# A decoder layer in split fp32r: the low parts of every fourth weight block formed by an accumulating transfer instead of VectorE

## The chip, the cores and the metric

One core of one Trainium2 chip runs the whole program. Its engines are TensorE (PE, matrix multiply; PEld is its weight load), VectorE (DVE), ScalarE (ACT), GpSimd (POOL) and SyncE (SP), which share an on-chip memory (SBUF); TensorE accumulates into PSUM banks. SP, ACT and POOL can each issue DMA transfers, which run on the core's 16 DMA engines. Every engine works through its own instructions in order and waits on semaphores for the others. The metric is the device time of one execution in microseconds (us).

## The reference

One layer of a decoder trunk with a sequence of 256 tokens, model width 2048, all in float32. The part that the change touches is the second half: a gated MLP and a gated embedding, both on RMS-normalised rows.

```python
h = rms_norm(x, mix_norm_g[i])
z = h @ w_in[i]
...
x = x + jnp.concatenate([ha, hb], axis=-1) @ w_out[i]
h = rms_norm(x, ffn_norm_g[i])
u = h @ w_up[i]
a, g = jnp.split(u, 2, axis=-1)
a = causal_dwconv(a, conv_w[i], conv_b[i])
x = x + (jax.nn.gelu(a, approximate=False) * g) @ w_down[i]
gate = jax.nn.sigmoid(rms_norm(x, ple_norm_g[i]) @ w_ple_gate[i])
x = x + gate * (p[i].astype(x.dtype) @ w_ple_proj[i])
```

The weights of these four products are `w_up` (2048 x 11264), `w_down` (5632 x 2048), `w_ple_gate` (2048 x 2048) and `w_ple_proj` (256 x 2048).

## The kernel before

Each weight matrix is streamed once from HBM in blocks of 128 partitions x 1024 float32 values (512 KB). To keep float32 accuracy on TensorE in its float32r format, each block is split in two: `hi` is the block rounded to float32r, `lo = raw - hi` is what the rounding left. The activations are split the same way (`split_T`, lines 139 to 149). A product is then three matmuls: hi times hi, lo times hi, hi times lo.

Two runs of `run_stream` (line 209) carry the whole layer: the first from `w_in` to `w_out`, the second from the up projection to the end. The second has 301 blocks: 176 of `w_up`, 88 of `w_down`, and 37 of `w_ple_proj` and `w_ple_gate`. For a block j the steps are

- SP loads it into a buffer `raw` (line 222), up to three blocks ahead in the loop (`AHEAD_DMA`),
- ACT writes `hi` (line 237), VectorE writes `lo` (line 239), up to three blocks ahead of TensorE (`AHEAD_SPLIT`),
- TensorE multiplies: `wide_group` (lines 317 and 318, the up projection), `token_group` (lines 267 to 269, the down projection, the gate and the projection of p), or `feature_group` (lines 293 to 295, first stream only).

The buffers set the pace of the look-ahead. There are three `raw` buffers (`RAW`) and four each of `hi` and `lo` (`PARTS`). A `raw` buffer comes free when both parts of its block have been formed; a `hi` or `lo` buffer when TensorE has finished its block. Which free buffer a new block gets, and the order of the instructions on each engine, are decided when the program is built, by a scheduler that estimates when each comes free; SP issues the loads strictly in the order of the blocks.

In the up projection a group of 8 blocks fills four PSUM banks; ACT and VectorE empty them (`merge`, `up_a`, `up_g`) between the splits of later blocks. The 22 groups each have a pair of offsets from the table `OFFS`: so many elements are the `hi` and the `lo` of its blocks shifted inside their buffers, which are 128 elements (`SLACK`) longer than a block. All other blocks have offset zero.

Of the kernel before, what the change touches and what calls it, by code (L numbers as in the profile page):

```python
# [10 lines left out]
F32R = mybir.dt.float32r  # L11
AF = mybir.ActivationFunctionType
ALU = mybir.AluOpType
AX = mybir.AxisListType

P = 128
# [7 lines left out]
FF = 5632  # L24
# [8 lines left out]
BLK = 1024  # L33
RAW, PARTS = 3, 4
AHEAD_DMA, AHEAD_SPLIT = 3, 3
PAD = 48
SLACK = 128

OFFS = [(0, 16), (16, 0), (0, 32), (16, 16), (0, 48), (32, 32), (0, 64), (16, 32), (48, 48), (0, 80), (32, 0),
        (0, 96), (16, 48), (64, 64), (0, 112), (64, 0), (8, 8), (32, 48), (48, 16), (64, 80), (8, 24), (0, 8)]  # L40


@with_exitstack
def layer_kernel(
# [7 lines left out]
    act, dve, pe, pool = nc.scalar, nc.vector, nc.tensor, nc.gpsimd  # L52
# [4 lines left out]
    wp = ctx.enter_context(tc.tile_pool(name="w", bufs=3))  # L57
# [5 lines left out]
    def f32(ap):  # L63
        return ap.bitcast(F32)
# [125 lines left out]
    def traced():  # L190

        return nc.cur_bb.bb.instructions[-1]
# [5 lines left out]
    def pull(n):  # L198

        while n > 0 and side:  # L200
            turn[0] ^= 1
            job = side[min(turn[0], len(side) - 1)]
            try:
                next(job)
                n -= 1
            except StopIteration:
                side.remove(job)

    def run_stream(blocks, pulls, ramp=False):

        nb = len(blocks)
        raws, parts = {}, {}
        split = 0
        for i in range(-AHEAD_DMA, nb):
            j = i + AHEAD_DMA
            if j < nb:
                src, _, _, load = blocks[j][:4]
                if load is not None:
                    load()
                kb, n = src.shape[1], src.shape[2]  # L220
                raws[j] = wp.tile([P, BLK], F32, tag="raw", name=f"raw{j}", bufs=RAW)
                nc.sync.dma_start(out=raws[j][:, : kb * n].rearrange("p (k n) -> p k n", k=kb), in_=src)

            ahead = min(AHEAD_SPLIT, 1 + i // 2) if ramp else AHEAD_SPLIT
            while i >= -1 and split < min(nb, i + ahead + 1):
                j, split = split, split + 1
                src, _, prep, _ = blocks[j][:4]
                if prep is not None:
                    prep()
                kb, n = src.shape[1], src.shape[2]  # L230
                w = kb * n
                raw = raws.pop(j)
                hi = wp.tile([P, BLK + SLACK], F32R, tag="hi", name=f"hi{j}", bufs=PARTS)
                lo = wp.tile([P, BLK + SLACK], F32R, tag="lo", name=f"lo{j}", bufs=PARTS)
                oh, ol = blocks[j][4] if len(blocks[j]) > 4 else (0, 0)
                hi, lo = hi[:, oh : oh + w], lo[:, ol : ol + w]
                act.copy(hi, raw[:, :w])  # L237
                last["hi"] = traced()
                dve.tensor_sub(lo, raw[:, :w], f32(hi))  # L239
                parts[j] = [v.rearrange("p (k n) -> p k n", k=kb) for v in (hi, lo)]  # L240
            if i >= 0:
                blocks[i][1](*parts.pop(i))
                pull(pulls)

    def wsrc(w, k0, kb, c0, n):
        return w[0, k0 * P : (k0 + kb) * P, c0 : c0 + n].rearrange("(k p) n -> p k n", p=P)
# [30 lines left out]
    def feature_group(w, c0, actT, finish):  # L277


        st = {}  # L280
        blocks = []
        for k0 in range(0, KD, 2):
            def fn(hi, lo, k0=k0):
                if k0 == 0:
                    st["b"] = [bank("mm", f"fg{j}").rearrange("p (j s) -> p j s", j=2) for j in range(2)]
                for j in range(4):
                    o = st["b"][j // 2][:, j % 2, :]
                    cols = slice(j * P, (j + 1) * P)
                    for i in range(2):
                        a = actT()[:, k0 + i, :]  # L290
                        first = k0 == 0 and i == 0 and j % 2 == 0
                        last = k0 == KD - 2 and i == 1 and j % 2 == 1
                        pe.matmul(o, hi[:, i, cols], a[:, 0:256], start=first, stop=False)  # L293
                        pe.matmul(o, hi[:, i, cols], a[:, 256:512], start=False, stop=False)  # L294
                        pe.matmul(o, lo[:, i, cols], a[:, 0:256], start=False, stop=last)  # L295
                    if k0 == KD - 2 and j % 2 == 1:
                        finish(j // 2, st["b"][j // 2])
            blocks.append((wsrc(w, k0, 2, c0, 512), fn, None, None))
        return blocks

    def wide_group(w, c0, actT, finish, tag, offs):


        st = {}
        blocks = []
        for k0 in range(0, KD, 2):
            def fn(hi, lo, k0=k0):
                if k0 == 0:
                    st["b"] = [bank(tag, f"wg{j}") for j in range(4)]
                for j in range(4):  # L310
                    o = st["b"][j]
                    cols = slice(j * P, (j + 1) * P)
                    for i in range(2):
                        a = actT()[:, k0 + i, :]
                        first = k0 == 0 and i == 0
                        last = k0 == KD - 2 and i == 1
                        pe.matmul(o, hi[:, i, cols], a, start=first, stop=False)  # L317
                        pe.matmul(o[:, 256:512], lo[:, i, cols], a[:, 0:256], start=False, stop=last)  # L318
                    if k0 == KD - 2:
                        finish(j, o)  # L320
            blocks.append((wsrc(w, k0, 2, c0, 512), fn, None, None, offs))
        return blocks

    apool = ctx.enter_context(tc.tile_pool(name="acts", bufs=1))
# [9 lines left out]
    with tc.tile_pool(name="mix", bufs=1) as mp:  # L334
# [328 lines left out]
        blocks = []  # L663
# [58 lines left out]
    with tc.tile_pool(name="ffn", bufs=1) as fp:  # L722
# [10 lines left out]
        def up_a(q):  # L733
            st = {}

            def f(jj, b):
                pair, j = divmod(jj, 2)
                if j == 0:
                    st["a"] = fp.tile([P, 2, S], F32, tag="a", name="a", bufs=2)
                    st["c"] = gl[q, pair] = fp.tile([P, 2, S], F32, tag="gl", name="c", bufs=3)  # L740
                a, c, k = st["a"], st["c"], 4 * q + jj
                merge(a[:, j], b)
                dve.tensor_mul(a[:, j], a[:, j], rb)
                act.activation(c[:, j], a[:, j], AF.Identity, scale=cT[:, 88 + k : 89 + k],
                               bias=cT[:, 132 + k : 133 + k])
                for d in (1, 2):
                    dve.scalar_tensor_tensor(out=c[:, j, d:S], in0=a[:, j, 0 : S - d],
                                             scalar=cT[:, 88 - 44 * d + k : 89 - 44 * d + k],
                                             in1=c[:, j, d:S], op0=ALU.mult, op1=ALU.add)
                if j == 1:  # L750
                    act.activation(c, c, AF.Gelu)
                    dve.tensor_mul(c, c, rb2)
            return f

        def up_g(q):
            st = {}

            def f(jj, b):
                pair, j = divmod(jj, 2)
                if j == 0:  # L760
                    st["u"] = fp.tile([P, 2, S], F32, tag="a", name="u", bufs=2)
                u, k = st["u"], 4 * q + 2 * pair
                merge(u[:, j], b)
                if j == 1:
                    dve.tensor_mul(u, u, gl.pop((q, pair)))
                    split_T(uT[:, k : k + 2, :], u)
            return f

        blocks = []
        x2 = aT["cur"]  # L770
        for q in range(KF // 4):
            blocks.extend(wide_group(w_up, q * 512, lambda: x2, up_a(q), "mm", OFFS[2 * q]))
            blocks.extend(wide_group(w_up, FF + q * 512, lambda: x2, up_g(q), "aux", OFFS[2 * q + 1]))
        ssq3 = sm.tile([P, NT, 4], F32, name="ssq3")
        x3T = {}

# [30 lines left out]
        for c0, n in ((0, 512), (512, 512), (1024, 512), (1536, 256), (1792, 256)):  # L807
            blocks.extend(token_group(w_ple_proj, [0], lambda: pT, c0, n, proj_done, tag="aux"))
            blocks.extend(token_group(w_ple_gate, all_k, get_x3T, c0, n, gate_done(c0, n, c0 == 1792)))
        run_stream(blocks, 0)  # L810


# [28 lines left out]
```

## Time and profile before

| | us |
|---|---|
| median of 2 runs (1292.0 to 1293.0) | 1292.5 |
| the profiled execution, whole | 1292.68 |
| its span, first to last instruction | 1291.0 |
| up projection, from 450.6 to 944.2 in the span | 493.6 |
| down projection, 944.2 to 1186.2 | 242.0 |
| gate, projection of p and the end, 1186.2 to 1291.0 | 104.8 |

The granted TensorE clock is 0.999 over the span. The span is one profiled execution; the 1.7 us between it and the whole lie around the program. All rows below come from that execution. Times in a row are microseconds unless marked ns; "x" and a number is a count of instructions; after a bar stand the busy time and the mean ns of one, and after the next bar the idle time of the engine just before them, with what ended it behind "<-".

### The profile page before, as it was taken

What the parts mean: (1) busy time and instruction counts of PE and PEld (TensorE: products, weight loads), DVE (VectorE), ACT (ScalarE), POOL (GpSimd) and SP (SyncE); (2) the same over time, 40 slices, a digit from 0 to 9 for tenths busy, and PEclk for the clock granted to TensorE, in tenths of its full rate; (3) what the DMA queues carried; (4) which work ended last, traced back from release to release, by engine and by line L of the source; (5) the groups of instructions that cost most, each with busy time, mean ns of one, the idle gap of its engine ahead of it and who ended that gap; (6) DMA issues with size and microseconds to landing.
All of it is one profiled execution on the core that took longest, in us unless ns stands there. A gap on an engine that the chain in (4) does not pass through costs nothing.

```text
span 1291.0 us, 18150 instructions
## 1 busy us (share of the span) xinstructions
PE 1284.0 (99%) x7060; PEld 1123.9 (87%) x7060; DVE 754.6 (58%) x1008; ACT 650.0 (50%) x964; POOL 18.4 (1%) x33
## 2 busy tenths in 40 slices
PE   9999999999999999999999999999999999999998
PEld 7899999988888888888888888888888888888888
DVE  5455566554565575766676576667654545455554
ACT  7655455435554464555455455545543434444443
POOL 2000000000000000000000000000000000000000
PEclk9999999999999999999999999999999999999999
DMA  8676755556655666666666666666656665565663
GB/s 248 175 189 188 217 151 144 159 144 171 177 184 185 186 180 194 184 191 184 192 190 185 188 188 185 190 187 190 191 193 191 191 192 186 193 191 192 203 204 123
DMA packets 132039, 238.69 MB, mean 185 GB/s; under 512 B 7945, under 2 KB 28017, under 8 KB 131953
## 3 DMA queue, kind: packets, MB, share of 16 engines
q1 hardware_dynamic: 131072, 237.07, 62.0%
q8 instruction: 55, 0.90, 0.3%
q10 hardware_dynamic: 657, 0.43, 0.1%
q0 software_dynamic: 224, 0.03, 0.1%
q14 instruction: 31, 0.25, 0.1%
HBM read 235.40 MB, written 2.10 MB: 184 GB/s over the span
## 4 chain that ended last, share of the span: by engine, by line
PE 98%; DMA 1%; DVE 0%; ACT 0%; issue 0%; SPq 0%; DVEq 0%
PE wg L317 25%; PE tg L268 17%; PE tg L269 17%; PE tg L267 17%; PE wg L318 13%; PE fg L293 2%; PE fg L295 2%; PE fg L294 2%; DMA raw<-in_w_in_dram 1%; PE xT L155 1%; PE mob L610 0%; PE msc L584 0%; PE qkp L508 0%; PE sc L524 0%; PE ob L549 0%; PE rowb L495 0%
## 5 line engine op out<-in xcount | busy, mean ns | idle before, releaser
L239 DVE TENSOR_TENSOR lo<-raw,hi 128x1024 fp32r<-128x1024 f32 (+2 forms) x462 | 546.7, 1184 | 478.4 <-ACT hi L237 476.1
L237 ACT CAST hi<-raw 128x1024 fp32r<-128x1024 f32 (+2 forms) x462 | 470.2, 1018 | 563.8 <-PE tg L269 283.2
L317 PE MATMUL wg<-x2T,hi 128*128 128x512 f32 x1408 | 492.5, 394 | 0.0
L318 PE MATMUL wg<-x2T,lo 128*128 128x256 f32 x1408 | 394.8, 281 | 0.0
L317 PEld LDWEIGHTS wg<-x2T,hi 128*128 128x128 f32 x1408 | 264.4, 188 | 60.9
L318 PEld LDWEIGHTS wg<-x2T,lo 128*128 128x128 f32 x1408 | 265.5, 189 | 0.1
L267 PE MATMUL tg<-hi,uT 128*128 128x512 f32 x352 | 137.2, 390 | 0.0
L269 PE MATMUL tg<-hi,uT 128*128 128x512 f32 x352 | 137.0, 389 | 0.0
L268 PE MATMUL tg<-lo,uT 128*128 128x512 f32 x352 | 137.0, 389 | 0.0
L268 PE MATMUL tg<-lo,hT 128*128 128x512 f32 (+1 forms) x384 | 136.6, 356 | 0.2 <-DVE lo L239 0.2
L267 PE MATMUL tg<-hi,hT 128*128 128x512 f32 (+1 forms) x384 | 136.0, 358 | 0.0
L269 PE MATMUL tg<-hi,hT 128*128 128x512 f32 (+1 forms) x384 | 135.6, 354 | 0.0
L268 PEld LDWEIGHTS tg<-lo,hT 128*128 128x128 f32 x384 | 72.2, 188 | 7.9 <-DVE lo L239 0.7
L269 PEld LDWEIGHTS tg<-hi,hT 128*128 128x128 f32 x384 | 72.1, 188 | 7.5
L267 PEld LDWEIGHTS tg<-hi,hT 128*128 128x128 f32 x384 | 71.8, 188 | 7.2 <-ACT hT L146 0.3
L269 PEld LDWEIGHTS tg<-hi,uT 128*128 128x128 f32 x352 | 66.1, 188 | 13.7
L267 PEld LDWEIGHTS tg<-hi,uT 128*128 128x128 f32 x352 | 66.1, 188 | 13.6
L268 PEld LDWEIGHTS tg<-lo,uT 128*128 128x128 f32 x352 | 66.1, 188 | 13.6
L293 PE MATMUL fg<-hT,hi 128*128 128x256 f32 x256 | 74.7, 292 | 0.0
L295 PE MATMUL fg<-hT,lo 128*128 128x256 f32 x256 | 73.1, 285 | 0.0
L294 PE MATMUL fg<-hT,hi 128*128 128x256 f32 x256 | 72.8, 284 | 0.0
L268 PE MATMUL tg<-lo,x3T 128*128 128x512 f32 (+1 forms) x160 | 55.5, 347 | 0.0
(212 smaller groups left out, 1186.6 us busy)
## 6 DMA issues: line engine op xcount, KB each, us to landing
raw<-in_w_up_dram SPq DMA_DIRECT2D x176, 512.0 KB, 4.2
raw<-in_w_down_dram SPq DMA_DIRECT2D x88, 512.0 KB, 4.8
raw<-in_w_in_dram SPq DMA_DIRECT2D x79, 512.0 KB, 3.8
raw<-in_w_in_dram SPq DMA_DIRECT2D x48, 344.0 KB, 3.4
raw<-in_w_out_dram SPq DMA_DIRECT2D x32, 512.0 KB, 4.2
raw<-in_w_ple_gate_dram SPq DMA_DIRECT2D x32, 512.0 KB, 4.8
xs<-in_x_dram SPq DMA_DIRECT2D x8, 256.0 KB, 7.8
raw<-in_w_ple_proj_dram SPq DMA_DIRECT2D x3, 512.0 KB, 4.7
```

The source lines that it names most:

```text
L155: pe.transpose(bk[:, t * P : (t + 1) * P], xs[:, t, k * P : (k + 1) * P], ident)
L237: act.copy(hi, raw[:, :w])
L239: dve.tensor_sub(lo, raw[:, :w], f32(hi))
L267: pe.matmul(o, ah, hi[:, i, :], start=first, stop=False)
L268: pe.matmul(o, ah, lo[:, i, :], start=False, stop=False)
L269: pe.matmul(o, al, hi[:, i, :], start=False, stop=last)
L293: pe.matmul(o, hi[:, i, cols], a[:, 0:256], start=first, stop=False)
L294: pe.matmul(o, hi[:, i, cols], a[:, 256:512], start=False, stop=False)
L295: pe.matmul(o, lo[:, i, cols], a[:, 0:256], start=False, stop=last)
L317: pe.matmul(o, hi[:, i, cols], a, start=first, stop=False)
L318: pe.matmul(o[:, 256:512], lo[:, i, cols], a[:, 0:256], start=False, stop=last)
```

## The change

From the up projection on, in every fourth block (j % 4 == 3, 75 of the 301), `lo` is formed without VectorE: ACT writes it a second time from `raw`, with scale -1 into float32r, which gives -hi; then POOL issues a transfer that adds `raw` onto it in SBUF. The other blocks are split as before. The table of offsets goes: `hi` always starts at the front of its buffer, which loses its slack, and `lo` is shifted by 16 elements in all blocks of `wide_group` and `feature_group`, and by none in those of `token_group`.

```diff
-SLACK = 128
...
-OFFS = [(0, 16), (16, 0), (0, 32), (16, 16), (0, 48), (32, 32), (0, 64), (16, 32), (48, 48), (0, 80), (32, 0),
...
+LO_SHIFT = 16
...
-    def run_stream(blocks, pulls, ramp=False):
+    def run_stream(blocks, pulls, ramp=False, by_dma=False):
...
-                hi = wp.tile([P, BLK + SLACK], F32R, tag="hi", name=f"hi{j}", bufs=PARTS)
-                lo = wp.tile([P, BLK + SLACK], F32R, tag="lo", name=f"lo{j}", bufs=PARTS)
-                oh, ol = blocks[j][4] if len(blocks[j]) > 4 else (0, 0)
-                hi, lo = hi[:, oh : oh + w], lo[:, ol : ol + w]
+                hi = wp.tile([P, BLK], F32R, tag="hi", name=f"hi{j}", bufs=PARTS)
+                lo = wp.tile([P, BLK + 128], F32R, tag="lo", name=f"lo{j}", bufs=PARTS)
+                hi, lo = hi[:, :w], lo[:, shift : shift + w]
                 act.copy(hi, raw[:, :w])
                 last["hi"] = traced()
-                dve.tensor_sub(lo, raw[:, :w], f32(hi))
+                if by_dma and j % 4 == 3:
+                    act.activation(lo, raw[:, :w], AF.Copy, scale=-1.0)
+                    pool.dma_start(out=lo, in_=raw[:, :w], accum_op=ALU.add)
+                else:
+                    dve.tensor_sub(lo, raw[:, :w], f32(hi))
...
-        run_stream(blocks, 0)
+        run_stream(blocks, 0, by_dma=True)
```

The instructions move at three places that matter. In the rows that follow, a number behind an underscore is a buffer's running name; in brackets stand the semaphores waited for: DMAHW and a digit is the landing of a transfer of SP's, DMASW and a digit that of one of POOL's, DVE, PE and Activation the progress of that engine.

SP's queue in the middle of the up projection, before:

```order
L222 DMA raw83_6458<-in_w_up_dram 128x2x512 [waits DMAHW6_49,DVE_49]
L222 DMA raw84_6484<-in_w_up_dram 128x2x512 [waits DMAHW7_49,DVE_49]
L222 DMA raw85_6506<-in_w_up_dram 128x2x512 [waits DMAHW0_49,DVE_49]
L222 DMA raw86_6528<-in_w_up_dram 128x2x512 [waits DMAHW1_49,DVE_49]
L222 DMA raw87_6550<-in_w_up_dram 128x2x512 [waits DMAHW2_49,DVE_49]
```

The same place of SP's queue in the change:

```order
L222 DMA raw83_6478<-in_w_up_dram 128x2x512 [waits DMAHW5_49,DMASW2_49]
L222 DMA raw84_6505<-in_w_up_dram 128x2x512 [waits DMAHW7_49,DVE_49]
L222 DMA raw85_6527<-in_w_up_dram 128x2x512 [waits DMAHW0_49,DVE_49]
L222 DMA raw86_6549<-in_w_up_dram 128x2x512 [waits DMAHW2_49,DVE_49]
L222 DMA raw87_6571<-in_w_up_dram 128x2x512 [waits DMAHW1_49,DMASW3_49]
```

Nothing changed its place, but the load of block 83 now waits for the landing of POOL's transfer of block 79 (lane 2) and that of block 87 for block 83's (lane 3), since they reuse those blocks' `raw` buffers. In 32 of the 44 such rounds of the up projection it is the load of block d+4 that waits for the transfer of block d, in 12 that of block d+3.

SP's queue in the down projection, in the change (before, each of these rows waits for a load's landing and DVE):

```order
L222 DMA raw202_9401<-in_w_down_dram 128x2x512 [waits DMAHW5_49,DMASW0_49,Activation_49]
L222 DMA raw203_9419<-in_w_down_dram 128x2x512 [waits DMAHW6_49,DVE_49]
L222 DMA raw204_9438<-in_w_down_dram 128x2x512 [waits DMAHW7_49,DVE_49]
L222 DMA raw205_9456<-in_w_down_dram 128x2x512 [waits DMAHW0_49,DVE_49]
L222 DMA raw206_9474<-in_w_down_dram 128x2x512 [waits DMAHW1_49,DMASW1_49,Activation_49]
```

Here, and in most rounds behind it, it is the load of block d+3 (202 for 199, 206 for 203) that waits, and the load of block d+4, itself one of the changed blocks, stands right behind it in the queue.

TensorE at block 83 of the up projection, before:

```order
L317 MATMUL wg0_6464<-x2T_3856,hi83_6460 128x512 [waits Activation_49]
L318 MATMUL wg0_6464<-x2T_3856,lo83_6461 128x256 [waits DVE_49]
L317 MATMUL wg0_6464<-x2T_3856,hi83_6460 128x512
L318 MATMUL wg0_6464<-x2T_3856,lo83_6461 128x256
L317 MATMUL wg1_6465<-x2T_3856,hi83_6460 128x512
```

TensorE at the same block in the change:

```order
L321 MATMUL wg0_6485<-x2T_3856,hi83_6480 128x512 [waits Activation_49]
L321 MATMUL wg1_6486<-x2T_3856,hi83_6480 128x512
L321 MATMUL wg2_6487<-x2T_3856,hi83_6480 128x512
L321 MATMUL wg3_6488<-x2T_3856,hi83_6480 128x512
L322 MATMUL wg0_6485<-x2T_3856,lo83_6481 128x256 [waits DMASW3_49]
```

The first matmul that reads the block's `lo` now waits for the landing of POOL's transfer, and one to three matmuls on `hi` of the other banks have moved ahead of it.

More of the change, by code (lines that the diff above doesn't have):

```diff
@@ L36 @@
 PAD = 48
-SLACK = 128
-OFFS = [(0, 16), (16, 0), (0, 32), (16, 16), (0, 48), (32, 32), (0, 64), (16, 32), (48, 48), (0, 80), (32, 0),
-        (0, 96), (16, 48), (64, 64), (0, 112), (64, 0), (8, 8), (32, 48), (48, 16), (64, 80), (8, 24), (0, 8)]
+LO_SHIFT = 16
 @with_exitstack
@@ L226, in run_stream @@
                 j, split = split, split + 1
-                src, _, prep, _ = blocks[j][:4]
+                src, _, prep, _, *shift = blocks[j]
+                shift = shift[0] if shift else 0
                 if prep is not None:
@@ L297, in fn, with wide_group @@
                         finish(j // 2, st["b"][j // 2])
-            blocks.append((wsrc(w, k0, 2, c0, 512), fn, None, None))
+            blocks.append((wsrc(w, k0, 2, c0, 512), fn, None, None, LO_SHIFT))
         return blocks
-    def wide_group(w, c0, actT, finish, tag, offs):
+    def wide_group(w, c0, actT, finish, tag):
         st = {}
@@ L320, in fn @@
                         finish(j, o)
-            blocks.append((wsrc(w, k0, 2, c0, 512), fn, None, None, offs))
+            blocks.append((wsrc(w, k0, 2, c0, 512), fn, None, None, LO_SHIFT))
         return blocks
@@ L771, in layer_kernel @@
         for q in range(KF // 4):
-            blocks.extend(wide_group(w_up, q * 512, lambda: x2, up_a(q), "mm", OFFS[2 * q]))
-            blocks.extend(wide_group(w_up, FF + q * 512, lambda: x2, up_g(q), "aux", OFFS[2 * q + 1]))
+            blocks.extend(wide_group(w_up, q * 512, lambda: x2, up_a(q), "mm"))
+            blocks.extend(wide_group(w_up, FF + q * 512, lambda: x2, up_g(q), "aux"))
         ssq3 = sm.tile([P, NT, 4], F32, name="ssq3")
```

## The prediction

> **What bounds the kernel now.** I read the page first (busy shares, then the chain of work that ended last), then the busy time by stage, then who waits for whom, then the transfers.
>
> ```profile
> PE 1284.0 (99%) x7060; PEld 1123.9 (87%) x7060; DVE 754.6 (58%) x1008; ACT 650.0 (50%) x964; POOL 18.4 (1%) x33
> PE 98%; DMA 1%; DVE 0%; ACT 0%; issue 0%; SPq 0%; DVEq 0%
> ```
>
> TensorE is busy 99% of the span and carries 98% of the chain. VectorE, which the change relieves, is busy 58% and has no share of the chain. So nothing is gained by doing its work elsewhere; the question is only whether TensorE is still fed.
>
> ```profile
> 450.60:944.20 493.60, 493.60 (x2829) 432.50 (x2828) 331.33 (x467) 263.66 (x358) 0.69 (x1) 1.00 0.65 188
> 944.20:1186.20 242.00, 242.00 (x1082) 200.63 (x1081) 119.84 (x115) 102.54 (x115) 0.00 (x0) 1.00 0.60 191
> 1186.20:1291.00 104.80, 100.56 (x550) 87.62 (x548) 54.24 (x64) 44.55 (x54) 0.70 (x1) 0.99 0.55 178
> ```
>
> These are the three stages of the second stream: length, then busy time of PE, PEld, DVE, ACT and POOL, the granted clock, the share and rate of the transfers. The up projection takes 493.6 / 176 = 2.80 us a block, the down projection 242.0 / 88 = 2.75 us; I take 2.75 us for the last stage too. Four blocks, one round of the change, are 11.2 us, then 11.0 us. That is the time in which the feeding must go round once.
>
> ```profile
> ACT hi L237 <- PE wg L317: 199.3, 154, 2.0
> SPq L222 <- DVE lo L239: 797.1, 363, 5.5
> 664.53 1.05 ACT L237 CAST hi<-raw 128x1024 fp32r<-128x1024 f32 x1 [1.00 <-PE wg L317]
> 667.30 1.05 ACT L237 CAST hi<-raw 128x1024 fp32r<-128x1024 f32 x1 [1.72 <-PE wg L317]
> 665.62 1.22 DVE L239 TENSOR_TENSOR lo<-raw,hi 128x1024 fp32r<-128x1024 f32 x1 [0.95 <-ACT hi L237]
> ```
>
> The waits (total, times, longest) show how the feeding turns today: ACT waits for TensorE to free a `hi` buffer, SP waits for VectorE to finish a `lo` and so free a `raw`. The timeline (start, duration) gives the steps: `hi` 1.05 us, 0.04 us of handing over, `lo` 1.22 us. A block's parts are ready about 2.3 us after TensorE frees their buffers, and TensorE comes to them three blocks, 8.4 us, later: 6.1 us of slack.
>
> **The change, part by part.** First its transfers, as the trace of before shows their kin: median us from issue to landing, then the load queue's total, then least, median and greatest for all loads of line 222.
>
> ```profile
> raw<-in_w_up_dram SPq DMA_DIRECT2D x176, 512.0 KB, 4.2
> raw<-in_w_down_dram SPq DMA_DIRECT2D x88, 512.0 KB, 4.8
> raw<-in_w_ple_gate_dram SPq DMA_DIRECT2D x32, 512.0 KB, 4.8
> g<-in_mix_norm_g_dram ACTq DMA_DIRECT2D x1, 8.0 KB, 2.5
> vrows<-in_ffn_norm_g_dram POOLq DMA_DIRECT2D x1, 8.0 KB, 3.5
> 1.41 0.69 POOL L94 DMA_DIRECT2D vrows<-in_ffn_norm_g_dram  x1 [0.32 <-issue]
> q1 hardware_dynamic: 131072, 237.07, 62.0%
> DMA to landing us min/median/max: 2.9/4.1/6.9
> ```
>
> *The landing of the new transfer, L.* No transfer of before adds, and none from POOL is large, so L is unknown. POOL's first transfer needs 3.5 us for 8 KB, of which POOL itself is busy 0.69 us; ACT's of 8 KB needs 2.5 us. The loads' own pace is 237.07 MB / (0.62 x 1291 us) = 0.296 MB per us, so 512 KB (0.524 MB) take 1.77 us. One pass over the data gives 3.5 + 1.77 = 5.3 us; a second pass, to fetch what is added onto, gives 7.0; a third 8.8. From below, a plain load of the same size lands in 4.2 us. I take 6.1 us, between one pass and two: the bytes don't come from HBM, but there are twice as many to read, and the loads run beside them at a share of 0.60 to 0.65. The ends 4.2 and 8.8 go into the range.
>
> The Trainium skill, "Collectives: The Full Stack" (The bandwidth ceiling: the fold count and why AG ≠ RS ≠ AR), says that an add in the DMA engines isn't slowed by the adding but by its two source reads on one queue, which halves the rate. No transfer of this trace tests that. By it L would be 7.0 us; what the sum becomes stands below as a rival.
>
> *Where L lies on the path.* The landing of block d frees its `raw` buffer, and SP holds the load that waits for it and all behind it. In 32 of the 44 rounds of the up projection that is the load of d+4, the next changed block. It closes a ring: landing of d, load of d+4 (4.2), `hi` (1.05), the negated copy on ACT (priced as the `hi` that reads and writes the same shapes, 1.05), five handovers of 0.04 (0.2), transfer L. One turn is 4.2 + 1.05 + 1.05 + 0.2 + 6.1 = 12.6 us, against TensorE's 11.2. Slack can't help a ring: each turn is late by the difference, so after the 6 us of slack are used, TensorE waits in every turn. In the other 12 rounds the load of d+3 waits and d+4's comes behind it, 1.77 us later: 14.4 us. In the down projection nearly all rounds are of that kind, with 4.8 us a load: 4.8 + 1.77 + 2.1 + 0.2 + 6.1 = 15.0 us against 11.0. In the last stage likewise.
>
> *The sum against the profiled execution.* Up: 32 x 12.6 + 12 x 14.4 = 576 us; in half of the 44 rounds a bank's copy (0.37 us, row below) stands on ACT between `hi` and the negated copy, 22 x 0.37 = 8; together 584, less 493.6: +90. Down: 22 x 15.0 = 330, less 242.0: +88. Last stage: 9 x (15.0 - 11.0) = +36. Sum +214 on 1292.7 us (0.2 us above the median): 1507 us.
>
> ```profile
> L730 ACT COPY a<-wg 128x256 f32<-128x256 f32 x44 | 16.3, 370 | 5.7 <-PE wg L318 5.7
> L239 DVE TENSOR_TENSOR lo<-raw,hi 128x1024 fp32r<-128x1024 f32 x296 | 362.5, 1225 | 315.4 <-ACT hi L237 313.9
> L237 ACT CAST hi<-raw 128x1024 fp32r<-128x1024 f32 x176 | 184.8, 1050 | 210.3 <-PE wg L317 199.1 <-ACT uT L143 6.9 <-issue 2.1
> ```
>
> *VectorE.* 75 x 1.225 = 92 us go; all of it lies beside TensorE, so 0. *ACT.* 75 x 1.05 = 79 us come, in its idle time (210 us before `hi` in the up projection alone); they count only in the ring above. What stands behind the negated copy is the next `hi`, which has slack. *POOL.* 75 issues of about 0.7 us; its only other work here is two tiny steps; the 0.7 is inside L. *The matmuls moved ahead* let TensorE begin a changed block on `hi` alone; they don't shorten the ring: 0. *Transfers.* One added transfer per four loads raises the bytes moved by a quarter to a half, so the share of 0.65 would go to about 0.81 to 0.97 at the old pace; it doesn't bound at the slower one.
>
> *The offsets.* Five groups of eight blocks of the up projection, the third, fourth, fifteenth, twenty-first and last:
>
> ```profile
> 496.50:518.70 22.20, 22.20 (x65) 12.03 (x65) 1.00 0.67 190
> 518.70:541.30 22.60, 22.60 (x65) 12.02 (x65) 1.00 0.66 185
> 765.70:788.10 22.40, 22.40 (x65) 12.03 (x65) 1.00 0.65 189
> 899.90:922.10 22.20, 22.20 (x66) 12.03 (x65) 1.00 0.65 190
> 922.10:944.20 22.10, 22.10 (x65) 11.88 (x64) 1.00 0.60 184
> ```
>
> With (0, 32), (16, 16), (0, 112), (8, 24) and (0, 8) a group takes 22.1 to 22.6 us; the mean is 493.6 / 22 = 22.4. One pair for all can win 22 x 0.3 = 7 us or lose 22 x 0.2 = 4. I take 0, since the ring leaves TensorE idle anyway.
>
> **The rivals.** *The ring stays inside TensorE's round, and nothing changes.* In the down projection it needs 8.9 + L below 11.0, so L below 2.1; for a loss within 2% (26 us; about what a measurement of this kernel can tell from no change) 31 x (8.9 + L - 11.0) = 26, so L up to 2.9. For it: the bytes stay on the chip. Against it: 2.9 us is the fastest load on record, and POOL's 8 KB took 3.5. It gives 1292 to 1318 us. 6 in 100. *Faster* would need TensorE itself to run faster; the offsets can give 7 us, 0.5%. 1 in 100 for more than 2%.
>
> *The adding reads twice and has no overlap, L = 7.0*: the turns grow by 0.9 us, 75 x 0.9 = 68, so 1575 us. For it: nothing shows that the second read is free. Against it: the 1.77 us is a rate from HBM. This is what the rule of the Trainium skill named above ("Collectives: The Full Stack") would make of it. 20 in 100.
>
> *The transfer is slow, L of 9 us and more*, because the add or POOL's writing of its steps costs more than passes over the data. With L = 12 every turn grows by 5.9 us: 75 x 5.9 = 443, so 1950 us. For it: no row has an add. Against it: POOL's issues cost only about 0.7 us. 13 in 100.
>
> **How the numbers follow.** The forecast, a ring paced by L of about 6, has 60 in 100: 1507 us. Its lower end, L = 4.2: the up projection loses only in the 12 long rounds, 12 x (12.5 - 11.2) = 16, the down projection 22 x (13.1 - 11.0) = 46, the last stage 19: 1374 us. Its upper end, L = 8.8: 75 x 2.7 = 203 more, 1710 us. The two-read case lies inside. The range 1375 to 1740 takes in the beginning of the slow case (L = 9.2) and leaves out some 19 in 100. Slower by over 2%: 60 + 20 + 13 = 93 in 100; within 2%: 6; faster: 1.
>
> **What would show it.** Right: in the profile of the changed kernel TensorE is idle some 200 us, all of it in the second stream, ahead of matmuls on `lo` and put down to POOL's transfer; SP waits for that transfer; a round lasts about 12.6 us in the up projection and 15 in the down projection; the transfer's row says 5.3 to 7. The first stream, to 450 us, is unchanged. The step on the order of loads is wrong if the down projection loses no more per round than the up projection; the price of L is wrong if its row lies outside 4.2 to 8.8. The whole is wrong if TensorE stays at 99% with rounds of 11 us: then the landing is below 3 us, or the load behind it isn't held.

## The result and the profile after

| | before | after |
|---|---|---|
| median, us | 1292.5 | 1392.35 (1390.8 to 1393.9) |
| ratio, 95% interval | | 1.0774 [1.0752, 1.0795] |
| the profiled execution: whole, span | 1292.68, 1291.0 | 1393.89, 1392.2 |

The change made the kernel 100 us slower. The forecast, 1507 us, had the direction, the place and the mechanism; it had the size at twice what came.

First the page of the kernel after: the busy time of each engine, and the shares of the chain that ended last.

```profile
PE 1305.9 (94%) x7060; PEld 1128.3 (81%) x7060; DVE 668.6 (48%) x933; ACT 702.5 (50%) x1039; POOL 82.2 (6%) x108
DMA 41%; PE 9%; ACT 7%; issue 4%; DVE 1%; SPq 1%; ACTq 0%; DVEq 0%; POOLq 0%
```

TensorE did the same 7060 matmuls, but the chain, which lay 98% on it before, now lies 41% on transfers. Of the 101.2 us by which the span grew, 79 are new idle time of TensorE (1392.2 - 1305.9 = 86.3, from 7.0) and 22 are matmuls that took longer (1305.9, from 1284.0).

The three stages of the second stream (length, then busy time of PE, PEld, DVE, ACT and POOL, granted clock, transfer share and rate):

```profile
449.40:968.60 519.20, 500.07 (x2830) 434.94 (x2829) 281.35 (x420) 290.63 (x399) 38.14 (x45) 0.99 0.80 222
968.60:1265.40 296.80, 252.87 (x1083) 201.93 (x1082) 93.00 (x92) 120.29 (x140) 18.70 (x22) 0.98 0.69 193
1265.40:1392.20 126.80, 106.29 (x549) 89.56 (x547) 45.03 (x56) 52.50 (x64) 8.38 (x10) 0.97 0.68 191
```

Against before the up projection is 25.6 us longer, the down projection 54.8, the last stage 22.0, and the first stream 1.2 shorter. Half as many blocks cost twice as much in the down projection. The waits say on what (engine and line, what it waited for: us in total, times, longest), TensorE's first:

```profile
PE tg L272 <- DMA lo<-raw: 57.7, 28, 3.5
PE wg L322 <- DMA lo<-raw: 19.0, 14, 2.2
```

```profile
SPq L222 <- DVE lo L243: 493.2, 213, 4.5
SPq L222 <- DMA lo<-raw: 339.9, 73, 7.8
```

76.7 of the 79 us stand ahead of matmuls on a `lo` that POOL's transfer forms, and SP holds its queue 73 times, once for nearly each of the 75 transfers, until one has landed. The ring itself is read from the chain, a stretch of the up projection first (start, duration, what):

```profile
731.39 3.83 DMA raw<-in_w_up_dram
...
735.33 1.06 ACT hi L237
736.38 0.27 ACT u L734
736.65 0.97 ACT lo L240
737.62 0.29 issue
737.91 4.75 DMA lo<-raw
...
742.68 4.22 DMA raw<-in_w_up_dram
```

One turn, from load to load, is 742.68 - 731.39 = 11.3 us: load, `hi`, a bank's copy (`u`), negated copy, transfer, and at once the next load. It is the ring of the forecast, with 4.75 in the place of 6.1. In the down projection it reads

```profile
1002.70 5.49 DMA raw<-in_w_down_dram
...
1008.29 1.08 ACT lo L240
1009.37 0.29 issue
1009.66 6.91 DMA lo<-raw
...
1016.64 0.37 SPq L222
...
1017.42 5.54 DMA raw<-in_w_down_dram
```

and one turn is 1017.42 - 1002.70 = 14.7 us. Here `hi` is missing: ACT makes the negated copy ahead of it. SP stands on the chain with the issue of the held load, which goes ahead of that of the changed block. A round, in the table, runs from the landing of one of POOL's transfers to that of the next, and L is that of the transfer that ends it. The trace has

| rounds | count | measured, us | forecast, us | transfer L, measured |
|---|---|---|---|---|
| up, load of d+4 held | 31 | 11.32 | 12.6 | 4.65 |
| up, load of d+3 held | 12 | 13.18 | 14.4 | 5.52 |
| down, d+3 held | 20 | 13.70 | 15.0 | 6.38 |
| down, d+4 held | 2 | 11.34 | 15.0 | |
| last stage, d+3 held | 7 | 13.91 | 15.0 | 6.13 |
| last stage, d+4 held | 2 | 10.85 | 15.0 | |

Why L is longer in the down projection shows in what moved during the two transfers of the chains above (packets, MB, share of 16 engines), 737.91 to 742.66 first, then 1009.66 to 1016.66:

```profile
q0 software_dynamic: 144, 0.52, 62.1%
q1 hardware_dynamic: 109, 0.19, 14.5%
```

```profile
q0 software_dynamic: 144, 0.52, 38.4%
q1 hardware_dynamic: 272, 0.52, 31.6%
```

POOL's 0.52 MB (q0) took about the same engine time in both, 0.621 x 4.75 = 2.95 us and 0.384 x 7.0 = 2.69 us of each engine. In the up projection 0.19 MB of loads (q1) ran in that time; in the down projection it was a whole block. Two runs below swap the conditions: where d+3 is held in the up projection too, the mean L there is 5.7 us (e4), and where d+4 is held in the down projection, 4.9 us (e9).

### The profile page after: what moved, and what is told of

It is laid out like the page before. It is cut to its first block, busy times and chain, and to the rows that moved or that the text cites. A ratio compares the mean times of both kernels' runs of the same rounds, so it can differ in the third digit from the quotient of the medians.

```text
span 1392.2 us, 18304 instructions
## 1 busy us (share of the span) xinstructions
PE 1305.9 (94%) x7060; PEld 1128.3 (81%) x7060; DVE 668.6 (48%) x933; ACT 702.5 (50%) x1039; POOL 82.2 (6%) x108
## 4 chain that ended last, share of the span: by engine, by line
DMA 41%; PE 9%; ACT 7%; issue 4%; DVE 1%; SPq 1%; ACTq 0%; DVEq 0%; POOLq 0%
DMA lo<-raw 23%; DMA raw<-in_w_down_dram 8%; DMA raw<-in_w_up_dram 8%; PE wg L321 5%; ACT lo L240 4%; DMA raw<-in_w_ple_gate_dram 3%; PE wg L322 3%; ACT hi L237 2%; PE tg L272 1%; PE tg L273 1%; PE tg L271 1%; SPq L222 1%; DVE lo L243 0%; DVE sg L805 0%; ACT x3T L145 0%
## 5 line engine op out<-in xcount | busy, mean ns | idle before, releaser
L243 DVE TENSOR_TENSOR lo<-raw,hi 128x1024 fp32r<-128x1024 f32 (+2 forms) x387 | 455.1, 1177 | 656.4 <-ACT hi L237 646.4
L321 PE MATMUL wg<-x2T,hi 128*128 128x512 f32 x1408 | 486.5, 395 | 0.0
L322 PE MATMUL wg<-x2T,lo 128*128 128x256 f32 x1408 | 381.0, 283 | 19.1 <-DMA lo<-raw 19.0
L322 PEld LDWEIGHTS wg<-x2T,lo 128*128 128x128 f32 x1408 | 269.4, 191 | 33.6 <-DMA lo<-raw 27.5
L272 PE MATMUL tg<-lo,uT 128*128 128x512 f32 x352 | 141.5, 402 | 42.6 <-DMA lo<-raw 42.6
L241 POOL DMA_DIRECT2D lo<-raw x75 | 63.8, 851 | 980.7 <-ACT lo L240 956.9
L240 ACT ACTIVATE lo<-raw 128x1024 fp32r<-128x1024 f32 (+1 forms) x75 | 79.1, 1055 | 16.7 <-DMA raw<-in_w_down_dram 7.6
L297 PE MATMUL fg<-hT,hi 128*128 128x256 f32 x256 | 74.3, 290 | 0.0
## 6 DMA issues: line engine op xcount, KB each, us to landing
xs<-in_x_dram SPq DMA_DIRECT2D x8, 256.0 KB, 7.6
```

The source lines that it names most:

```text
L240: act.activation(lo, raw[:, :w], AF.Copy, scale=-1.0)
L241: pool.dma_start(out=lo, in_=raw[:, :w], accum_op=ALU.add)
L272: pe.matmul(o, ah, lo[:, i, :], start=False, stop=False)
```

## The experiments

The theory of the ring: a `raw` buffer is held until a transfer has landed, SP's queue stands behind it, and so a round lasts as long as load, ACT's pieces and transfer together. Its rivals: the transfers crowd the DMA engines; ACT's second pass delays the splits; the matmuls themselves got slower by the placement of `hi` and `lo`. All results (stages by the first matmul of each; the ratio is to the kernel before, run on the same chip, 1292.3 to 1292.7 us):

| run | median, us | ratio to before, 95% interval | up, down, last, us |
|---|---|---|---|
| e1_offsets_alone | 1287.04 | 0.9960 [0.9945, 0.9975] | 489.5, 242.1, 104.6 |
| e12_no_shift | 1298.16 | 1.0041 [1.0026, 1.0056] | 498.7, 242.1, 104.6 |
| e8_one_pair | 1293.13 | 1.0005 [0.9996, 1.0014] | 494.2, 242.1, 104.6 |
| e5_plain_copy | 1329.92 | 1.0286 [1.0272, 1.0300] | 490.5, 270.0, 117.0 |
| e3_raw4 | 1302.92 | 1.0084 [1.0069, 1.0099] | 494.3, 243.1, 114.6 |
| e13_raw4_neg_first | 1307.65 | 1.0116 [1.0099, 1.0132] | 498.7, 245.2, 113.0 |
| e4_neg_first | 1431.30 | 1.1073 [1.1055, 1.1092] | 557.5, 297.8, 125.8 |
| e2_own_raw | 1439.61 | 1.1143 [1.1126, 1.1161] | 531.5, 319.9, 132.3 |
| e6_own_raw_neg_first | 1442.62 | 1.1166 [1.1149, 1.1183] | 534.9, 321.5, 132.2 |
| e9_own_raw_in_order | 1335.88 | 1.0339 [1.0304, 1.0374] | 508.5, 256.0, 114.0 |
| e11_own_raw_in_order_neg | 1327.57 | 1.0271 [1.0254, 1.0288] | 499.7, 259.9, 113.0 |

e7_quiet was run once, for its transfers alone. Edits are against the kernel after unless said otherwise.

### The two halves of the change apart

e1 keeps the new placement of `hi` and `lo` and drops the transfers:

```diff
-        run_stream(blocks, 0, by_dma=True)
+        run_stream(blocks, 0, by_dma=False)
```

> The new placement of the parts without any accumulating transfer: every low part is formed by VectorE. Prediction on record: the offsets are worth 0, between -7 and +4 us, so 1286 to 1297 us. Rival: the placement carries a good part of the 100 us, because TensorE's reads meet other accesses at the new addresses; then 1310 us or more, with longer rounds of the up projection at TensorE busy 99%.

Measured 1287.04, as expected: the placement alone gains 5.2 us, and the transfers, with ACT's second pass for them, cost 1392.35 - 1287.04 = 105 us. TensorE is never idle in its up projection (length, then PE's busy time):

```profile
449.60:939.10 489.50, 489.50 (x2830) 432.94 (x2829) 331.10 (x467) 264.46 (x358) 0.70 (x1) 1.00 0.65 189
```

So the same 2830 matmuls took 4.1 us less than before at the same clock. Two more runs looked for the reason. e12 is e1 without the shift; e8 is the kernel before with one pair for all groups:

```diff
-LO_SHIFT = 16
+LO_SHIFT = 0
```

```diff
-            blocks.extend(wide_group(w_up, q * 512, lambda: x2, up_a(q), "mm", OFFS[2 * q]))
+            blocks.extend(wide_group(w_up, q * 512, lambda: x2, up_a(q), "mm", (8, 24)))
```

(and the like for the other half of the columns.)

> The new placement without accumulating transfers, as in the run that took 1287 us, with the low part shifted by 0 in place of 16 elements. If the shift of the low part is what gains the 5 us, the up projection goes back to 493 to 497 us and the time to 1291 to 1296 us; if the shorter hi buffers (other addresses) do, it stays at 1287 us.

> The kernel before with the pair of offsets (8, 24) for all 22 groups of the up projection in place of the table. That pair's group took 22.2 us where the mean was 22.4. If the placement sets TensorE's pace, the up projection falls by 22 x 0.25 = 5 us, to 1287 us; if the differences between groups come from something else that changes from group to group, the time stays at 1292.5.

Without the shift the up projection takes 498.7 us, 9.2 more than with it; the whole came out above both figures expected, so the shift gains 11 us, and the shorter buffers without it lose 5.5 to the kernel before. One pair for all groups changes nothing (494.2 against 493.6), the second of the two outcomes named, although the pair (8, 24) belongs to one of the fast groups of before. The pace of a group isn't its pair's alone. In the built programs of the kernel before, e1 and e12 the instructions of TensorE, VectorE, ACT and SP stand in the same order, so what differs is where the parts lie; which part of that TensorE feels wasn't separated.

### The price of one transfer

e7 is the kernel before with six transfers of one block behind all other work, each waiting for the one ahead, three that add and three that copy:

```diff
+        for _ in range(3):
+            pool.dma_start(out=dst, in_=src, accum_op=ALU.add)
+        for _ in range(3):
+            pool.dma_start(out=dst, in_=src)
```

> The kernel before with six transfers of POOL's added behind its end, one after the other, 128 x 1024 elements each from SBUF to SBUF: three that add, then three that copy, with nothing else on the DMA engines. If the add's second read costs, the adding ones land in 4.0 to 4.5 us and the copying ones 1.0 to 1.3 us sooner; if it costs nothing, all six land alike. In both cases the adding ones land sooner than the 4.7 and 6.4 us of the changed kernel by what the loads beside them cost. The end of the program gets later by six landings, some 25 us; its time says nothing else.

POOL's timeline of the four later ones, two that add, then two that copy (start, duration of the issue, in brackets the wait ahead of it):

```profile
1295.85 0.90 POOL L820 DMA_DIRECT2D qdst<-qsrc  x1 [4.07 <-DMA qdst<-qsrc]
1300.59 0.85 POOL L820 DMA_DIRECT2D qdst<-qsrc  x1 [3.84 <-DMA qdst<-qsrc]
1305.30 0.56 POOL L822 DMA_DIRECT2D qdst<-qsrc  x1 [3.86 <-DMA qdst<-qsrc]
1308.47 0.54 POOL L822 DMA_DIRECT2D qdst<-qsrc  x1 [2.61 <-DMA qdst<-qsrc]
```

From issue to issue an add takes 1305.30 - 1300.59 = 4.7 us, a copy 3.1 to 3.2; from issue to landing the trace has 4.4 to 4.5 and 2.8 to 2.9. The add came as expected, the copy 1.6 us sooner instead of 1.0 to 1.3: POOL's issue of an add is itself 0.3 us longer. In the kernel after the same add took 4.75 us (median) in the up projection and 6.7 in the down projection, so up to 2.2 us come from what runs beside it.

e5 leaves out the adding alone, so that `lo` of the changed blocks is `raw` itself:

```diff
-                    pool.dma_start(out=lo, in_=raw[:, :w], accum_op=ALU.add)
+                    pool.dma_start(out=lo, in_=raw[:, :w])
```

> As the changed kernel, but POOL's transfer copies raw over the low part in place of adding, so the low part of every fourth block is raw itself, not what the rounding left. Same bytes written, same buffers, same waits; nothing is read of what is added onto. If the second read is what makes a packet of 4 KB take 0.33 us in the changed kernel, eight packets an engine get shorter by up to half, 1.3 us, and the landing falls from 4.7 to about 3.5 us in the up projection and from 6.4 to about 5.2 in the down projection: rounds of 11.2 to 12 us in the up projection and about 12.4 in the down projection, 1320 to 1350 us in all. Rival: the landing is fixed cost and queueing behind the loads, the add costs nothing: landing and time as in the changed kernel, 1380 to 1400 us.

Measured 1329.92, as expected; the landing is 2.9 us in the up projection and 5.5 in the down projection (medians), where 3.5 and 5.2 were expected. POOL's queue, in the kernel after and in e5:

```profile
q0 software_dynamic: 11024, 39.09, 15.2%
```

```profile
q0 software_dynamic: 11024, 39.09, 8.1%
```

For the same packets and bytes the engines were busy 0.152 x 1392.2 = 212 us with the add and 0.081 x 1326.0 = 107 us without, 1.97 times as long. That is what the Trainium skill says in "Collectives: The Full Stack" (The bandwidth ceiling: the fold count and why AG ≠ RS ≠ AR) of the adds of a collective: an add costs two source reads and so half the rate; these two rows agree. The stages of e5:

```profile
448.50:939.00 490.50, 490.50 (x2830) 432.81 (x2829) 282.23 (x421) 297.77 (x402) 24.57 (x45) 1.00 0.73 236
939.00:1209.00 270.00, 250.59 (x1083) 201.64 (x1082) 92.13 (x92) 119.64 (x136) 11.88 (x22) 0.99 0.66 210
```

With L at 2.9 the short ring of the up projection would last 11.32 - 4.65 + 2.9 = 9.6 us (an estimate), against TensorE's 490.5 / 44 = 11.15, and TensorE is never idle. The down projection still loses 28 us: there the copy needs 5.5 us, the second load stays in the ring, and the mean round is 12.45 us.

### The buffer that the transfer holds

e3 gives `raw` a fourth buffer. Room for it comes from the slack of `lo`, so the shift goes too; its counterpart without transfers is e12, not e1.

```diff
-RAW, PARTS = 3, 4
+RAW, PARTS = 4, 4
...
-LO_SHIFT = 16
+LO_SHIFT = 0
...
-                lo = wp.tile([P, BLK + 128], F32R, tag="lo", name=f"lo{j}", bufs=PARTS)
+                lo = wp.tile([P, BLK], F32R, tag="lo", name=f"lo{j}", bufs=PARTS)
```

> As the changed kernel, with four raw buffers in place of three (and no shift of the low parts, which makes the room; the shift is worth 0 by the prediction). The landing of block d then holds the load of d+4 or d+5. Theory of the ring: where d+5 is held there is no ring of one round any more, where d+4 is held it is as long as TensorE's round: 1290 to 1305 us. Rival, the transfers themselves: as many and as large as before, so 1370 to 1395 us.

Measured 1302.92, within what the ring expects, with every transfer and every pass of ACT still there. Its stages and the only large wait of TensorE:

```profile
451.40:945.70 494.30, 494.30 (x2830) 431.40 (x2829) 284.46 (x423) 303.07 (x402) 38.14 (x45) 1.00 0.83 234
945.70:1188.80 243.10, 242.79 (x1082) 200.45 (x1081) 93.39 (x92) 122.23 (x137) 18.70 (x22) 1.00 0.79 235
1188.80:1303.40 114.60, 103.85 (x549) 88.29 (x547) 43.28 (x54) 51.84 (x63) 8.39 (x10) 0.98 0.71 206
```

```profile
PE tg L272 <- DMA lo<-raw: 6.8, 6, 2.6
```

The up projection runs without a pause at a transfer share of 0.83, higher than the 0.80 of the kernel after; the down projection loses 1 us. So neither the crowding of the engines nor ACT's second pass costs the 105 us: 1302.92 - 1298.16 = 4.8 us are left of them against e12. By stages e3 is 4.4 us shorter than e12 in the up projection, where neither lets TensorE wait but the buffers lie elsewhere, 1.0 longer in the down projection and 10.0 longer in the last stage. So what the transfers still cost is some 11 us, nearly all in the last stage, where TensorE waits 6.5 us for them. A stretch of its chain:

```profile
1203.96 0.24 PE tg L272
1204.22 1.07 ACT lo L240
1205.29 0.29 issue
1205.59 5.89 DMA lo<-raw
1211.52 0.50 PE tg L272
...
1215.27 6.70 DMA lo<-raw
1222.02 4.54 DMA raw<-in_w_ple_gate_dram
1226.67 1.07 ACT lo L240
1227.74 0.28 issue
1228.02 6.05 DMA lo<-raw
1234.11 0.50 PE tg L272
```

Two rings stand here in turn. In the first five rows TensorE's last matmul on an old `lo` frees the buffer, ACT fills it, the transfer adds, and TensorE comes to it 7.3 us later: the four `lo` buffers are the next bound. In the last six a load still goes out at the landing of a transfer (1215.27 + 6.70 = 1221.97), the ring of before. What each of them costs wasn't separated.

e13 is e3 with SP's loads held to the order of the blocks and the negated copy made ahead of `hi`:

```diff
+                if by_dma and j % 4 == 3:
+                    act.activation(lo, raw[:, :w], AF.Copy, scale=-1.0)
+                    with tc.issue_after(traced()):
+                        act.copy(hi, raw[:, :w])
...
+                if by_dma and "raw" in last:
+                    with tc.issue_after(last["raw"]):
+                        nc.sync.dma_start(out=dst, in_=src)
```

> Four raw buffers, loads in the order of the blocks, and the negated copy first: every landing holds the load of d+4, with a ring of about 10 to 10.9 us under TensorE's round everywhere. If the ring is all that the transfers cost, the time is that of the same placement without them (the run with no shift beside this one) within 5 us in the first two stages; if their traffic or ScalarE's second pass costs by itself, some 10 us more, as the run with four raw buffers (1303 us) leaves open.

1307.65, 4.7 us above e3: the shorter way to the transfer gains nothing where the ring is open already. Nearly all of the 4.7 us is the up projection, 498.7 us without a wait, the same as e12's. So the first of the two outcomes holds where it was stated: 0.0 and 3.1 us above e12 in the first two stages. Its last stage, 113.0 us, is hardly nearer to the 104.6 of e12 than e3's 114.6, so at most 1.6 us of that remainder come from the order on ACT and SP; the rest stays open.

### The order on the queues

e4 makes only the first of these two edits, in the kernel after: the negated copy ahead of `hi`.

> As the changed kernel, with ScalarE's negated copy ahead of the copy to hi in every fourth block. The down projection has that order already; in the up projection it takes 1.05 us out of the ring. But by the order of the instructions every landing in the up projection now holds the load of d+3, where before 32 of 44 held d+4. Theory of the ring with what the changed kernel's rounds show (0.5 us to the issue behind the held load, 5.2 for the second load, 0.2, 1.05, 0.3 to POOL, 5.5 for the transfer): 12.8 us a round in the up projection, so 530 to 565 us there against 519, and 1400 to 1440 us in all: slower, though ScalarE's path is shorter. Rival, ScalarE's second pass is what costs: faster than the changed kernel by up to 44 x 1.05 = 46 us, 1345 to 1390 us.

1431.30, as expected, and 39 us slower than the kernel after, although ACT's part of the ring got 1.05 us shorter. With that edit the scheduler hands the buffers out differently: now every landing of the up projection holds the load of d+3, with that of d+4 behind it, and the mean round is 12.68 us. The whole loss is in the up projection (557.5 against 519.2), where 31 of 43 rounds were of the short kind.

e2 takes the changed blocks out of the common buffers: one `raw` of their own, two for the others.

```diff
-                raws[j] = wp.tile([P, BLK], F32, tag="raw", name=f"raw{j}", bufs=RAW)
+                own = j % 4 == 3
+                raws[j] = wp.tile([P, BLK], F32, tag="rawd" if own else "raw", name=f"raw{j}", bufs=1 if own else RAW - 1)
```

> As the changed kernel, but the blocks that are formed by transfer (every fourth) have one raw buffer of their own and the other blocks two, in place of three for all; the memory is the same. Every landing then holds the load of block d+4, never that of d+3. Theory of the ring (the landing of block d, the load held for it, ScalarE, the next transfer): the rounds in which d+4 was held took 11.3 us in the up projection and 10.9 to 11.3 later, against 13.2 to 13.9 where d+3 was held, so all rounds fall to about TensorE's 11.2 and 11.0: up projection 494 to 505 us, down projection 242 to 250, last stage 105 to 110, in all 1292 to 1312 us. Rival, the transfers themselves (a share of the DMA engines of 0.70 to 0.80, the second pass of ScalarE, loads that land 0.1 to 0.4 us later): nothing of that is taken away, so 1370 to 1395 us.

1439.61: 128 us above the highest figure expected. SP's queue in the down projection tells why (a load, and in brackets the landings and engines that it waits for; DMASW is a transfer of POOL's):

```
L223 DMA raw201_9381<-in_w_down_dram 128x2x512 [waits DMAHW5_49,DVE_49]
L223 DMA raw203_9419<-in_w_down_dram 128x2x512 [waits DMAHW4_49,DMASW0_49,Activation_49]
L223 DMA raw202_9401<-in_w_down_dram 128x2x512 [waits DMAHW6_49,DVE_49]
L223 DMA raw204_9438<-in_w_down_dram 128x2x512 [waits DMAHW7_49,DVE_49]
```

The scheduler had put the load of 203, which waits for the landing of 199's transfer, ahead of that of 202, which waits for no transfer of POOL's. So the queue held both, and a block that needs no transfer waited for one. By the semaphores in the trace this order stands in 18 of the 22 rounds of the down projection and in 12 of the 43 of the up projection. e6 adds the negated copy ahead of `hi` to it, and meets the same order:

> The raw buffer of its own for every fourth block and the negated copy ahead of the copy to hi, together. Theory of the ring: 0.02 + 3.9 + 0.1 + 1.05 + 0.3 + 4.7 = 10.1 us in the up projection and 10.9 in the down projection, both under TensorE's round: TensorE waits nowhere, 1288 to 1298 us, within 2% of the kernel before and not faster, since TensorE bounds both. Rival, the transfers themselves: 1345 us or more.

1442.62, the same miss. e9 is e2 with one thing more, the second edit shown under e13: each load is issued after the one of the block before it.

> The raw buffer of its own for every fourth block again, now with SP's loads pinned to the order of the blocks; where they were left to the scheduler, it had put the held load of d+4 ahead of that of d+3 in every round of the down projection and in a part of those of the up projection, so that d+3 came late as well. Theory of the ring: the landing holds d+4 and nothing that is needed sooner; the rounds that already stood so took 11.1 to 11.3 us. Up projection 490 to 505 us, down projection 242 to 252, last stage 105 to 116, 1287 to 1315 us. If the two buffers that are left to the other blocks are what made 1440 us, the time stays above 1400 us; if the transfers themselves cost, above 1370 us.

1335.88, 104 us faster than e2 with the same buffers, transfers and work, and 56 faster than the kernel after, in the same memory. The order of one queue was worth 104 us, and the time lies below the 1345 us (e6) and 1370 us (e9) named for the case that the transfers themselves cost. It is still 21 us above what was expected. The mean rounds are 11.7 us in the up and 11.5 us in the down projection, since the ring through the one buffer has no reserve: L is 4.8 at the median and 7.1 at most, and each slow one is lost. The five transfers over 6 us had 0.5 to 1.0 MB of loads beside them, the other 70 in the median 0.34 MB, so the loads beside a transfer are the likely cause; it isn't shown by an edit. Of the 45 us by which its span exceeds e1's, 26 are idle time of TensorE and 17 are matmuls that took longer (1296.9, from 1280.0); the cause of the latter wasn't separated. With the negated copy ahead of `hi` as well,

> The same with the negated copy ahead of the copy to hi in the up projection too: the ring there shrinks from about 11.2 to about 10.1 us, under TensorE's 11.1. Theory: 1287 to 1305 us, the up projection 0 to 10 us shorter than with the copy to hi first. Rival, the transfers themselves: no gain over the run with the copy to hi first, and above 1370 us.

the up projection is 8.8 us shorter, inside the 0 to 10 expected, but the down projection is 3.9 us longer, and the whole, 1327.57, stays above 1305.

The fastest kernel of the study is e1, which has no transfers: 1287.04 us.

## Why the prediction was right in kind and wrong in size

**That TensorE has to be fed, and VectorE's relief is worth nothing: right.** VectorE lost 86 us of work (754.6 to 668.6), and no stage gained. e1, with VectorE's full work, is 105 us faster.

**The ring through `raw`: right, and shown by an edit.** A fourth buffer takes nearly all of the loss away (e3), a worse order of the loads adds to it (e2, e4), buffers dealt out otherwise, with the loads in order, take half of it away (e9). The steps named for the profile came: the idle time lies ahead of matmuls on `lo`, SP waits for the transfers, the down projection loses more per round than the up projection, the first stream is as before. The amounts didn't come: TensorE was idle 79 us more and not some 200, and the rounds lasted 11.3 and 13.7 us and not 12.6 and 15. L was to be judged by its row:

```profile
lo<-raw POOLq DMA_DIRECT2D x74, 512.0 KB, 5.3
```

That lies inside the 4.2 to 8.8 named, but it is one median over all stages, 4.75 in the up and 6.7 in the down projection, and so was too coarse a sign to catch the step that failed.

**The price of L in the up projection: the step that failed.** It was put at 6.1, between 3.5 + 1.77 and a second pass, and was 4.65 in the 31 short rounds (those where d+4 is held) and 5.52 in the 12 long ones. The fixed part, 3.5 us, came from POOL's first transfer of 8 KB at the start of the program. In e7 a whole copy of 512 KB, issue included, takes 2.9 us, so a fixed part of 3.5 can't be. The second read was priced about right (1.77 us a pass; the add is 1.6 longer than the copy).

The rounds came out 1.28 and 1.22 us shorter than forecast: 31 x 1.28 + 12 x 1.22 = 54 of the 64 us that were too many (90 forecast, 25.6 measured). In the short rounds L alone is 1.45 less, and the handovers are a little more. In the long ones L is 0.58 less; most of the rest is the second load, which goes out 0.5 us behind the held one where 1.77 was put. The 8 us put down on top for the banks' copies on ACT came in part: they stand in 21 of the short rounds and delay each by 0.26 us, and the measured rounds contain them.

Why so little was lost is chance. The short ring, 4.16 for the load and the wait behind it, 1.05 + 0.08 + 1.06 on ACT, 0.32 for handovers and 4.65 for L, lasts 11.32 us; TensorE's round, in e1 with the same placement, is 489.5 / 44 = 11.13. So the short rounds lose 31 x 0.19 = 6 us and the long ones 12 x (13.18 - 11.13) = 25, against the 29.7 us by which the up projection is longer than e1's.

**The down projection: the path and two terms of the ring.** L was about right (6.38 for 6.1). But the path was wrong: `hi` isn't in the ring, since ACT's order there has the negated copy first (the order is fixed when the program is built, so it could have been read beforehand): -1.05. The two loads behind each other took 0.55 + 5.22 = 5.77 us for 6.57: -0.80. Handovers were 0.55 for 0.2: +0.35. With L's +0.28 a round is 1.2 us less, over 20 rounds 24 us, and the 2 rounds of the other kind are 3.7 each below: 31 of the 33 us missed. The last stage, +22 for +36, was taken for nine long rounds of 15.0 and had seven, of 13.9.

**The offsets at 0: inside their bounds, by a wrong reason.** The placement gained 5.2 us (bounds 7 won, 4 lost). But the bounds were read from groups as if their pairs made their pace, and e8 says that they don't.

**The load on the DMA engines doesn't bound: right** (e3, 0.83 with no idle time). **The matmuls moved ahead at 0: not tried by itself.**

**The rivals.** That the adding reads twice fits the engines' time (1.97 times the copy's, e5), and the rival still was wrong in its 1575 us, since it took over the same fixed part of 3.5. A hidden ring needed L below 2.9; a plain copy just reaches that in the up projection (e5), the add doesn't.

## What to carry to other kernels

Before a transfer takes over work that an engine did, write down which buffer its landing frees, which load waits for that buffer and what stands behind that load in its queue: that closed turn, against the time of the blocks it feeds, is the price, and one buffer more or another order of the loads can be worth more than the transfer itself. Count the turn from the order of each engine at that very stage, since the same source lines gave two orders on ACT here. And a small first transfer at the start of a program is a poor measure of the fixed part of a large one in the middle.

## What was unexpected in the hardware

**The granted clock fell after short gaps.** The kernel before ran at 0.999. In the kernel after, the clock was 0.50 in seven stretches, six of 3.4 us and one of 6.8; two of them (length, busy time of PE, PEld, DVE, ACT and POOL, clock, share, rate):

```profile
919.90:923.30 3.40, 3.40 (x12) 2.97 (x12) 1.18 (x2) 1.86 (x4) 0.00 (x0) 0.50 0.80 252
1015.50:1022.30 6.80, 5.69 (x13) 4.46 (x14) 1.21 (x2) 1.04 (x1) 0.00 (x0) 0.50 0.60 184
```

TensorE's timeline at the first of them (in brackets the gap ahead):

```profile
919.71 0.43 PE L322 MATMUL wg<-x2T,lo 128*128 128x256 f32 x1 [2.09 <-DMA lo<-raw]
919.93 0.63 PE L321 MATMUL wg<-x2T,hi 128*128 128x512 f32 x1
```

Each stretch begins between 1.2 us before and 1.5 us after the end of a gap of 1.85 to 3.3 us, and a matmul that takes 0.40 us elsewhere takes 0.63. The Trainium skill, "TensorE: Matmul & The Clock Gate" (What's actually happening), speaks of an idle window of about 3.4 us; the stretches have that length, but gaps shorter than it were enough here, at times, while one of 3.49 us (ahead of 1194.82) left the clock alone. By an estimate, 25 us of busy time at half speed cost about 13 of the 22 us by which TensorE's busy time grew; the rest wasn't separated.

**TensorE's pace depends on where its operands lie.** The same matmuls of the up projection, without idle time and at clock 1.00, took 489.5, 493.6 and 498.7 us in e1, the kernel before and e12, with the instructions in the same order; only the places of the parts differ.

**An adding transfer** from POOL costs 1.97 times the engine time of a copy and 0.85 us of POOL for 0.54; alone it lands in 4.4 to 4.5 us (e7), beside a load's 0.52 MB in 6.9 (the chain above).
